# A planner that orders a two-layer encoder's instructions, given other durations and a convolution handed out one step at a time

## The chip, the cores and the metric

The kernel runs on one core of a Trainium2 chip. A core has TensorE (PE in the rows, with PEld for its weight loads), VectorE (DVE), ScalarE (ACT), GpSimd (POOL) and SyncE (SP), which here only issues DMAs. The metric is device time in microseconds of one execution; the kernel before has a median of 2336.31 over three runs.

## The reference

Two layers of a bidirectional encoder over 1024 tokens of width 1024. In each, five branches of width 256 run on the same normalised input, each is projected back to 1024 columns, weighted by a sigmoid gate and added, and the sum goes through an output projection. The branch that matters here is the convolution module:

```python
def conformer_branch(a, b, z, w_dw, b_dw, ln_g, ln_b):
    u = a * jax.nn.sigmoid(b)
    c = (depthwise_conv(u, w_dw) + b_dw.astype(u.dtype)).astype(F32)   # 31 taps
    mu = jnp.mean(c, axis=-1, keepdims=True)
    var = jnp.mean(jnp.square(c - mu), axis=-1, keepdims=True)
    n = (c - mu) * lax.rsqrt(var + EPS) * ln_g.astype(F32) + ln_b.astype(F32)
    return jax.nn.silu(n).astype(a.dtype) * jax.nn.silu(z)

for l in range(DEPTH):
    h = rmsnorm(x, norm_pre[l])
    ...                       # 18 projections of h; hgrn2, conformer, short conv, window and memory attention
    for n, yb in enumerate((y_hg, y_cf, y_sc, y_at, y_mem)):
        term = jax.nn.sigmoid(h @ w_gate[l, n]) * (yb @ w_branch[l, n])
        merged = term if merged is None else merged + term
    x = x + rmsnorm(merged @ w_out[l], norm_post[l])
```

## The kernel before

Channels lie on the 128 partitions, tokens along the free axis, in two halves of 512 (`s` is 0 or 1). A float32 product is made of three products of rounded parts (high by high, low by high, high by low), type float32r, each 128 rows by 512 columns: these are the split products. Scores, scan and value products of the attentions are plain float32 matmuls on 64 rows or 64 columns of the array, and transposes go through PE too.

All five engines run in the order in which the program emits, which the program decides while it is built. A main stream of items (projections, branch products, gates) emits one after the other on PE; beside it stand side generators (`plan.side`): recurrence, attention workers, convolution, preparation of gate operands. Class `Meter` (line 74 on) wraps each engine and gives every instruction an assumed duration, `cost`; class `Planner` keeps an assumed clock per engine and, per tile, when it was written and read. After each group of three products the main stream calls `plan.poll()`, which resumes every side generator that is due: `due` is the time at which its last piece is assumed to be seen (its end plus 0.2 us), or, for generators with `idle="DVE"`, the assumed end of VectorE's queue if that is later; it must not lie after PE's assumed clock. A generator emits up to its next `yield`. No instruction is timed by the plan on the chip; the durations only decide who stands before whom.

The convolution is such a generator with `idle="DVE"` (`conv` in `conformer_items`). For each of the two channel groups `j` it emits one tensor_scalar for the middle tap and 30 scalar_tensor_tensor, one per further tap, all on VectorE into `cf_c`; it yields after every odd tap, so two taps are emitted per resumption. Then come, for each half `s`, the sum over both groups (`cf_sum`), its split into `cf_muh` (ACT) and `cf_mul` (DVE), two products with a matrix of 1/256 (`cf_mu` on PE, the mean), the subtraction, squares on ACT, again a split and two products (`cf_var`), the root (ACT, with a table load), the reciprocal (DVE), a scale, a tanh (ACT, with a table load) and two more steps per group. The two halves are emitted one after the other. Only then the flag `cf` of the layer is set.

The main stream around it: `mem` (memory attention projections `ps_mq`, `ps_m_z`), `hz` (`ps_hz`), the first gate of branch 2 (`sc_g[:1]`, tiles `ps_g`), the products of branch 0 (`ps_b`), the three further gates (`sc_g[1:]`, 144 products into `ps_g`), and then `cz` (`ps_cz`), the projection whose SiLU multiplies the convolution's result. `cz` has `need=f"cf{l}"`: before its body the program calls `plan.wait`, which lets PE's assumed clock jump to the next due side piece until the flag is set. So whatever is left of the convolution's chain when the main stream reaches `cz` is emitted there, ahead of `ps_cz` on PE, with no other product between. After `cz` come branches 3, 1 and 4, then the gates as 7-product Strassen groups (`ps_gX`, `ps_gY`, `ps_gZ`), then the output projection.

Since `Meter` issues everything, nearly all rows carry one line number, L112; the tiles tell the rows apart.

Of the kernel before, what the change touches and what calls it, by code (L numbers as in the profile page):

```python
# [12 lines left out]
F32R = mybir.dt.float32r  # L13
# [62 lines left out]
class Meter:  # L76


    def __init__(self, engine, key, plan):
        self.engine, self.key, self.plan = engine, key, plan  # L80

    def __getattr__(self, name):
        f = getattr(self.engine, name)

        def call(*args, **kw):
            given = list(args) + [v for k, v in kw.items() if k not in ("out", "accum_out")]
            outs = [kw[k] for k in ("out", "accum_out") if k in kw]
            if "out" not in kw:
                outs.append(given.pop(0))
            tiles = [x for x in given if hasattr(x, "tensor")]  # L90
            n = prod(outs[0].shape[1:])
            if self.key == "PE":
                if name == "transpose":
                    cost = 0.107
                elif kw["rhs"].dtype == F32R:
                    cost = max(0.107, 0.00042 * n)
                else:
                    tiled = outs[0].shape[0] <= HD or kw["lhsT"].shape[0] <= HD
                    cost = max(0.085, 0.00167 * n) * (0.65 if tiled else 1.0)
            elif self.key == "DVE":  # L100
                n = max([n] + [prod(x.shape[1:]) for x in tiles])
                each = {"reciprocal": 0.0063, "tensor_scalar": 0.0006, "tensor_copy": 0.0006}.get(name, 0.00107)
                cost = (0.1 if name == "scalar_tensor_tensor" else 0.065) + n * each + 0.1 * ("accum_out" in kw)
            elif self.key == "ACT":
                cost = 0.055 + n * 0.00087 + 0.22 * ("accum_out" in kw) + self.plan.table(kw.get("func"))
            elif self.key == "DMA":
                cost = prod(outs[0].shape) * 1.12e-5
            else:
                cost = 0.05 + n * 0.0008 if name == "memset" else 0.5
            self.plan.add(self.key, cost, [x.tensor.name for x in outs],  # L110
                          [x.tensor.name for x in tiles])
            return f(*args, **kw)  # L112

        return call


class Planner:


    def __init__(self):  # L120
        self.t = dict.fromkeys(("PE", "DVE", "ACT", "POOL", "DMA"), 0.0)
        self.written, self.read = {}, {}
        self.last = 0.0
        self.flags = set()
        self.sides = []
        self.rings = {}
        self.loaded = None

    def add(self, key, cost, outs, ins):
        t = self.t[key]  # L130
# [76 lines left out]
def encoder(ctx: ExitStack, tc: tile.TileContext, a: dict, out: bass.AP):  # L207
# [398 lines left out]
    def conformer_items(l, hT, cs):  # L606
# [11 lines left out]
        def conv():  # L618
            yield f"at{l}01"
            for j in range(2):  # L620
# [6 lines left out]
                for k in range(CONFK):  # L627
                    if k == mid:
                        continue
                    o = k - mid  # L630
                    dst = c[:, max(0, -o):T - max(0, o)]
                    src = u[:, max(0, o):T - max(0, -o)]
                    dve.scalar_tensor_tensor(out=dst, in0=src, scalar=wt[:, j, k:k + 1], in1=dst,
                                             op0=ALU.mult, op1=ALU.add)
                    if k % 2:
                        yield
            for s in range(2):
                both = h2("cf_sum")
                dve.tensor_tensor(out=both, in0=cs[0][:, hs(s)], in1=cs[1][:, hs(s)], op=ALU.add)
# [23 lines left out]
            plan.flags.add(f"cf{l}")  # L663

        plan.side(conv(), idle="DVE")
        res = []
        for j in range(2):
# [895 lines left out]
```

## Time and profile before

| | us |
|---|---|
| median of 3 runs (2334.42 to 2337.20) | 2336.31 |
| the profiled execution's own time | 2335.37 |
| its span in the trace | 2333.6 |
| PE busy in the span | 2247.9 |
| DVE busy | 1644.3 |
| ACT busy | 996.4 |
| granted TensorE clock, mean share of full | 0.987 |

A matmul row's length counts its passage through the array, 0.39 us for 512 columns, while the next one starts 0.23 us later; what a product costs in a stream is the distance between starts. An engine's idle time stands in brackets behind a row, with what ended it.

### The profile page before, as it was taken

The numbers are of one execution on the slowest core, as the hardware profiler recorded it, in microseconds if no ns is written. First come the engines' busy times: TensorE is split into PE (matmuls) and PEld (weight loads), VectorE is DVE, ScalarE is ACT, GpSimd is POOL, SyncE is SP. The second block draws the span as 40 slices with busy tenths as digits, with TensorE's granted clock in tenths as the row PEclk, the third lists the DMA queues.
The fourth block names the chain that finished last, engine by engine and source line by source line (L and its number), as shares of the span: only waits on it lengthen the run. The fifth ranks groups of instructions, "written<-read, shape, count | busy, mean of one in ns | idle before, by whom it ended". The sixth has DMA issues, their size and how long they took to land.

```text
span 2333.6 us, 30426 instructions
## 1 busy us (share of the span) xinstructions
PE 2247.9 (96%) x11488; PEld 1837.7 (79%) x11488; DVE 1644.3 (70%) x2870; ACT 996.4 (43%) x1982; POOL 27.3 (1%) x41
## 2 busy tenths in 40 slices
PE   7999999989989999999999999999998999999998
PEld 6777788878767888887887878887786788888876
DVE  6767634788784887878667686266886768877765
ACT  5333344354455333335542424344544643333342
POOL 1000000000000000000110000000000000000000
PEclk9899999999999999999999999999999999999999
DMA  7102031101427333325450010411023463332244
GB/s 200 47 14 73 28 124 37 52 10 37 149 108 246 116 131 109 109 90 190 163 128 28 28 37 19 142 44 37 28 74 116 162 207 128 109 108 91 92 152 163
DMA packets 244563, 228.96 MB, mean 98 GB/s; under 512 B 29600, under 2 KB 190624, under 8 KB 244416
## 3 DMA queue, kind: packets, MB, share of 16 engines
q1 hardware_dynamic: 244416, 227.01, 29.7%
q8 instruction: 91, 1.49, 0.3%
q14 instruction: 56, 0.46, 0.1%
HBM read 173.49 MB, written 53.48 MB: 97 GB/s over the span
## 4 chain that ended last, share of the span: by engine, by line
PE 85%; DVE 8%; ACT 4%; issue 2%; DMA 0%; SPq 0%; POOL 0%; DVEq 0%; ACTq 0%; POOLq 0%
PE ps_gY L112 12%; PE ps_gX L112 8%; PE ps_b L112 8%; PE ps_gZ L112 8%; PE ps_o L112 7%; PE ps_hf L112 4%; PE ps_g L112 3%; PE h_s L112 3%; PE ps_cb L112 2%; PE ps_ca L112 2%; PE ps_hz L112 2%; PE ps_sc L112 2%; PE ps_sz L112 2%; PE ps_aq L112 2%; PE ps_at_z L112 2%
## 5 line engine op out<-in xcount | busy, mean ns | idle before, releaser
L112 DVE TENSOR_TENSOR lo<-raw_g,hi 128x512 fp32r<-128x512 f32 x232 | 159.0, 688 | 116.7 <-ACT hi L112 116.7
L112 ACT CAST hi<-raw_g 128x512 fp32r<-128x512 f32 x232 | 141.9, 616 | 60.5 <-PE ps_gY L112 56.2
L112 DVE SCALAR_TENSOR_TENSOR cf_c<-cf_u,cfw,cf_c 128x1009 f32<-128x1009 f32 (+14 forms) x120 | 152.9, 1274 | 2.7
L112 DVE TENSOR_TENSOR lo<-raw_in,hi 128x512 fp32r<-128x512 f32 x120 | 77.4, 686 | 94.9 <-ACT hi L112 94.8
L112 PE MATMUL ps_b<-yh,hi 128*128 128x512 f32 x320 | 125.9, 394 | 4.5 <-ACT pb_out L112 2.2
L112 PE MATMUL ps_b<-yl,hi 128*128 128x512 f32 x320 | 125.1, 391 | 1.4 <-DVE yl L112 1.4
L112 PE MATMUL ps_b<-yh,lo 128*128 128x512 f32 x320 | 124.7, 390 | 0.0
L112 ACT COPY pb_out<-ps_b 128x512 f32<-128x512 f32 x160 | 91.6, 590 | 77.3 <-PE ps_b L112 68.3
L112 ACT ACTIVATE g_e<-g_e 128x512 f32<-128x512 f32 x72 | 45.6, 634 | 161.3 <-DVE g_e L112 161.3
L112 PE MATMUL ps_gX<-h_0h,hi 128*128 128x512 f32 x288 | 112.1, 389 | 0.0
L112 PE MATMUL ps_gX<-h_0h,lo 128*128 128x512 f32 x288 | 112.1, 389 | 0.0
L112 PE MATMUL ps_gX<-h_0l,hi 128*128 128x512 f32 x288 | 112.0, 389 | 0.0
L112 PEld LDWEIGHTS h_s<-hQQ,hkp 64*128 64x128 f32 x896 | 60.9, 192 | 25.8 <-issue 18.2
L112 ACT CAST hi<-raw_in 128x512 fp32r<-128x512 f32 x120 | 68.8, 619 | 27.4 <-PE ps_ca L112 17.3
L112 PE MATMUL h_s<-hQQ,hkp 64*128 64x128 f32 x896 | 73.4, 298 | 6.4 <-DVE hQQ L112 2.5
L112 DVE TENSOR_TENSOR lo<-raw_wo,hi 128x512 fp32r<-128x512 f32 x64 | 42.2, 687 | 47.9 <-PE ps_o L112 28.5
L112 PEld LDWEIGHTS ps_b<-yh,hi 128*128 128x128 f32 x320 | 60.1, 188 | 19.7 <-ACT pb_out L112 4.0
L112 DVE COPY_PREDICATED hS<-masks,h_s 128x512 f32<-128x512 uint8 x112 | 75.3, 726 | 0.0
L112 PEld LDWEIGHTS ps_b<-yl,hi 128*128 128x128 f32 x320 | 60.1, 188 | 15.8 <-DVE yl L112 3.2
L112 ACT COPY hkp<-hK 128x512 f32<-128x512 f32 x56 | 37.2, 664 | 80.9 <-DVE hK L112 80.9
L112 PEld LDWEIGHTS ps_b<-yh,lo 128*128 128x128 f32 x320 | 60.1, 188 | 11.9
L112 ACT CAST hi<-raw_wo 128x512 fp32r<-128x512 f32 x64 | 37.8, 621 | 60.9 <-PE ps_o L112 47.0
(558 smaller groups left out, 6457.5 us busy)
## 6 DMA issues: line engine op xcount, KB each, us to landing
pb<-pb_out SPq DMA_DIRECT2D x160, 256.0 KB, 2.3
raw_g<-in_w_gate_dram SPq DMA_DIRECT2D x80, 512.0 KB, 3.6
pb<-pb SPq DMA_DIRECT2D x80, 512.0 KB, 5.2
raw_in<-in_w_in_dram SPq DMA_DIRECT2D x68, 512.0 KB, 3.8
raw_wo<-in_w_out_dram SPq DMA_DIRECT2D x32, 512.0 KB, 4.6
raw_b<-in_w_branch_dram SPq DMA_DIRECT2D x20, 512.0 KB, 4.1
x<-in_x_dram SPq DMA_DIRECT2D x8, 512.0 KB, 7.5
raw_mkv<-in_w_mem_kv_dram SPq DMA_DIRECT2D x8, 512.0 KB, 4.8
```

Source lines behind the costliest of these rows:

```text
L112: return f(*args, **kw)
```

## The change

Three of the assumed durations on PE change (split products from at least 0.107 us and 0.00042 us per column to 0.0135 + 0.000418 per column; plain matmuls from at least 0.085 to at least 0.212, tiled ones at 0.7 of it and no longer 0.65), and 0.09 us is added whenever a split product follows one that isn't, or the other way round. On VectorE the fixed part is larger for three kinds of instruction. And the convolution yields after every tap. No instruction is added, removed or altered by that; 27 loads of activation tables become 22, since these follow from the order on ScalarE.

```diff
             if self.key == "PE":
+                split = name != "transpose" and kw["rhs"].dtype == F32R
                 if name == "transpose":
                     cost = 0.107
-                elif kw["rhs"].dtype == F32R:
-                    cost = max(0.107, 0.00042 * n)
+                elif split:
+                    cost = 0.0135 + 0.000418 * n
                 else:
                     tiled = outs[0].shape[0] <= HD or kw["lhsT"].shape[0] <= HD
-                    cost = max(0.085, 0.00167 * n) * (0.65 if tiled else 1.0)
+                    cost = max(0.212, 0.00167 * n) * (0.7 if tiled else 1.0)
+                cost += 0.09 * (split != self.plan.split)
+                self.plan.split = split
             elif self.key == "DVE":
                 n = max([n] + [prod(x.shape[1:]) for x in tiles])
-                each = {"reciprocal": 0.0063, "tensor_scalar": 0.0006, "tensor_copy": 0.0006}.get(name, 0.00107)
-                cost = (0.1 if name == "scalar_tensor_tensor" else 0.065) + n * each + 0.1 * ("accum_out" in kw)
+                each = {"reciprocal": 0.0063, "tensor_scalar": 0.0005, "tensor_copy": 0.0006}.get(name, 0.00107)
+                fixed = {"scalar_tensor_tensor": 0.16, "tensor_scalar": 0.23, "copy_predicated": 0.12}.get(name, 0.07)
+                cost = fixed + n * each + 0.1 * ("accum_out" in kw)
...
         self.loaded = None
+        self.split = True
...
                     dve.scalar_tensor_tensor(out=dst, in0=src, scalar=wt[:, j, k:k + 1], in1=dst,
                                              op0=ALU.mult, op1=ALU.add)
-                    if k % 2:
-                        yield
+                    yield
```

What it moves, at three places (the helper's line is L116 in the changed program) of the first layer (the second has the same pattern at the first two). The first is PE at the gates of branch 2 (`ps_g`, operands `h_0h` and so on are the normalised input's parts) and the mean and variance products. Before, the first half's mean stands in the middle of a gate:

```order
L112 MATMUL ps_g_5432<-h_0l_111,hi 128x512
L112 MATMUL ps_g_5432<-h_0h_108,hi 128x512
L112 MATMUL ps_g_5432<-h_0h_108,lo 128x512
L112 MATMUL ps_g_5432<-h_0l_112,hi 128x512
L112 MATMUL cf_mu<-cf_muh,mean_w 128x512
L112 MATMUL cf_mu<-cf_mul,mean_w 128x512
L112 MATMUL ps_g_5432<-h_0h_108,hi 128x512
L112 MATMUL ps_g_5432<-h_0h_108,lo 128x512
```

Of the 144 products of these gates 81 stand behind that `cf_mu`, and 57 behind the first `cf_var`; only the second half's pairs stand between the last gate and `ps_cz`. With the change:

```order
L116 MATMUL ps_g_5520<-h_1h_260,lo 128x512
L116 MATMUL ps_g_5520<-h_1l_264,hi 128x512
L116 MATMUL cf_mu<-cf_muh,mean_w 128x512
L116 MATMUL cf_mu<-cf_mul,mean_w 128x512
L116 MATMUL cf_var<-cf_varh,mean_w 128x512
L116 MATMUL cf_var<-cf_varl,mean_w 128x512
L116 MATMUL cf_mu<-cf_muh,mean_w 128x512
L116 MATMUL cf_mu<-cf_mul,mean_w 128x512
L116 MATMUL cf_var<-cf_varh,mean_w 128x512
L116 MATMUL cf_var<-cf_varl,mean_w 128x512
L116 MATMUL ps_cz<-h_0h_106,hi 128x512
L116 MATMUL ps_cz<-h_0h_106,lo 128x512
```

Both halves' mean and variance products now stand behind the last gate, with nothing between them, ahead of `ps_cz`.

The second place is VectorE in the same stretch. `cf_c_4676` before and `cf_c_5106` now are the convolution of the second channel group, `mg` and `g_th` the merging of a gate with its branch, `lo` the low part of a weight. Before, the last taps and the first half's sum:

```order
L112 SCALAR_TENSOR_TENSOR cf_c_4676<-cf_u_3553,cfw_921,cf_c_4676 128x1011
L112 SCALAR_TENSOR_TENSOR cf_c_4676<-cf_u_3553,cfw_921,cf_c_4676 128x1010
L112 SCALAR_TENSOR_TENSOR mg_5031<-mg_5031,pb 128x512
L112 SCALAR_TENSOR_TENSOR cf_c_4676<-cf_u_3553,cfw_921,cf_c_4676 128x1009
L112 TENSOR_TENSOR cf_sum<-cf_c_3599,cf_c_4676 128x512
L112 TENSOR_TENSOR cf_mul<-cf_sum,cf_muh 128x512
L112 SCALAR_TENSOR_TENSOR mg_5075<-mg_5075,pb 128x512
L112 TENSOR_TENSOR lo<-raw_g_5355,hi 128x512 x2
```

Now the same sum and what stands ahead of it:

```order
L116 SCALAR_TENSOR_TENSOR g_th<-g_th,pb 128x512
L116 SCALAR_TENSOR_TENSOR cf_c_5106<-cf_u_3553,cfw_949,cf_c_5106 128x1011
L116 SCALAR_TENSOR_TENSOR cf_c_5106<-cf_u_3553,cfw_949,cf_c_5106 128x1010
L116 SCALAR_TENSOR_TENSOR cf_c_5106<-cf_u_3553,cfw_949,cf_c_5106 128x1009
L116 SCALAR_TENSOR_TENSOR g_th<-g_th,pb 128x512
L116 TENSOR_TENSOR lo<-raw_in_1920_5487,hi 128x512 x2
L116 TENSOR_TENSOR cf_sum<-cf_c_3596,cf_c_5106 128x512
L116 TENSOR_TENSOR cf_mul<-cf_sum,cf_muh 128x512
```

The last taps moved behind the merging of the fourth gate's first half, and the sum behind the merging of its second half, which needs the last gate product. Of this group's 30 further taps 18 stood behind the merging of the first gate's second half before, now 29 do.

The third place is PE in the projection `ps_hz`, beside the memory attention (`m_s` scores, `m_t` transposes, `m_o` products with the values, from two workers). Before:

```order
L112 MATMUL ps_hz<-h_1l_261,hi 128x512
L112 MATMUL m_t<-ident,m_p 128x128 x8
L112 MATMUL ps_hz<-h_1h_258,hi 128x512
L112 MATMUL ps_hz<-h_1h_258,lo 128x512
L112 MATMUL ps_hz<-h_1l_262,hi 128x512
L112 MATMUL m_o<-m_pT,mV_678 64x128 x8
L112 MATMUL ps_hz<-h_1h_258,hi 128x512
```

Now:

```order
L116 MATMUL ps_hz<-h_1l_261,hi 128x512
L116 MATMUL m_t<-ident,m_p 128x128 x4
L116 MATMUL ps_hz<-h_1h_258,hi 128x512
L116 MATMUL ps_hz<-h_1h_258,lo 128x512
L116 MATMUL ps_hz<-h_1l_262,hi 128x512
L116 MATMUL m_t<-ident,m_p 128x128 x4
L116 MATMUL m_o<-m_pT,mV_678 64x128 x4
L116 MATMUL ps_hz<-h_1h_258,hi 128x512
L116 MATMUL ps_hz<-h_1h_258,lo 128x512
L116 MATMUL ps_hz<-h_1l_262,hi 128x512
L116 MATMUL m_o<-m_pT,mV_678 64x128 x4
```

The two workers no longer stand side by side: runs of eight transposes and eight value products became two of four each. Over the whole program, runs of value products between other kinds go from 50 to 62, runs of transposes from 90 to 107, and those of the 64-row products (`h_s` and the like) stay at 57. The Strassen groups and the output projection keep their order on PE.

## Rows read from the trace of the kernel before

**Rows 1.** The page's span and busy time of each engine, and the first line of its chain of work that ended last, by engine.

```profile
span 2333.6 us, 30426 instructions
...
PE 2247.9 (96%) x11488; PEld 1837.7 (79%) x11488; DVE 1644.3 (70%) x2870; ACT 996.4 (43%) x1982; POOL 27.3 (1%) x41
...
PE 85%; DVE 8%; ACT 4%; issue 2%; DMA 0%; SPq 0%; POOL 0%; DVEq 0%; ACTq 0%; POOLq 0%
```

**Rows 2.** Busy time of each engine in stretches of the span; the columns are the stretch, its length, the engines with their instruction counts, the granted TensorE clock as a share of full, the DMA engines' share and GB/s. The recurrence lies in 20 to 310 and 1187 to 1457, the attentions in 460 to 570 and 1605 to 1716, the end of the convolution's chain in 640 to 665 and 1786 to 1812.

```profile
20.00:120.00 100.00, 92.60 (x583) 77.14 (x583) 69.67 (x140) 39.85 (x86) 3.73 (x6) 0.93 0.34 84
120.00:310.00 190.00, 183.26 (x1123) 145.58 (x1122) 134.42 (x240) 72.14 (x126) 0.00 (x0) 0.99 0.11 34
...
460.00:570.00 110.00, 102.29 (x635) 82.74 (x634) 85.74 (x210) 55.91 (x164) 0.00 (x0) 0.98 0.09 30
...
640.00:665.00 25.00, 17.14 (x60) 13.01 (x61) 17.10 (x23) 9.25 (x14) 0.00 (x0) 0.80 0.22 74
...
1187.00:1280.00 93.00, 90.51 (x596) 73.55 (x595) 69.11 (x122) 34.86 (x71) 4.88 (x4) 1.00 0.31 77
1280.00:1457.00 177.00, 170.53 (x1065) 138.34 (x1064) 125.72 (x224) 69.84 (x123) 0.00 (x0) 1.00 0.10 30
...
1605.00:1716.00 111.00, 104.12 (x634) 84.41 (x633) 86.75 (x214) 55.51 (x160) 0.00 (x0) 0.95 0.09 29
...
1786.00:1812.00 26.00, 17.92 (x64) 13.35 (x63) 17.43 (x24) 9.92 (x14) 0.00 (x0) 0.80 0.21 71
```

**Rows 3.** Instructions on PE in order of time, from the last gate product to the first product of `ps_cz`, first layer; columns are start, length, engine, line, operation, tiles, shapes, and in brackets the idle time before with what ended it.

```profile
639.11 0.39 PE L112 MATMUL ps_g<-h_1l,hi 128*128 128x512 f32 x1
644.45 0.79 PE L112 MATMUL cf_mu<-cf_muh,mean_w 128*128 128x512 f32 x1 [4.95 <-ACT cf_muh L112]
...
649.38 0.80 PE L112 MATMUL cf_var<-cf_varh,mean_w 128*128 128x512 f32 x1 [3.42 <-ACT cf_varh L112]
...
650.70 0.63 PE L112 MATMUL ps_cz<-h_0h,hi 128*128 128x512 f32 x1
```

**Rows 4.** The same view of VectorE, second half's sum to the end of the chain.

```profile
641.26 0.68 DVE L112 SCALAR_TENSOR_TENSOR g_th<-g_th,pb 128x512 f32<-128x512 f32 x1
...
643.06 0.68 DVE L112 TENSOR_TENSOR cf_sum<-cf_c,cf_c 128x512 f32<-128x512 f32 x1
...
650.94 0.69 DVE L112 TENSOR_SCALAR cf_rs<-cf_var 128x512 f32<-128x512 f32 x1 [0.89 <-PE cf_var L112]
...
662.03 0.69 DVE L112 SCALAR_TENSOR_TENSOR cf_c<-cf_t,cf_c 128x512 f32<-128x512 f32 x1
662.64 0.68 DVE L112 TENSOR_TENSOR b<-h_1h,h_1l 128x512 f32<-128x512 f32 x1
```

**Rows 5.** The same view of ScalarE; the first row is the tanh of the last gate.

```profile
639.94 0.57 ACT L112 ACTIVATE g_th<-ps_g 128x512 f32<-128x512 f32 x1
...
643.78 0.62 ACT L112 CAST cf_muh<-cf_sum 128x512 fp32r<-128x512 f32 x1 [2.24 <-DVE cf_sum L112]
...
656.48 1.28 ACT L112 ACT_TABLE_LOAD   x1 [4.19 <-DVE cf_c L112]
657.78 0.82 ACT L112 ACTIVATE cf_t<-cf_c,cfh 128x512 f32<-128x512 f32 x1
```

**Rows 6.** The same view of all engines where the first half's chain lies; `SPq` and `PEld` rows are left out.

```profile
613.97 0.69 DVE L112 TENSOR_TENSOR cf_sum<-cf_c,cf_c 128x512 f32<-128x512 f32 x1
...
620.07 0.39 PE L112 MATMUL cf_mu<-cf_muh,mean_w 128*128 128x512 f32 x1
...
620.53 0.39 PE L112 MATMUL ps_g<-h_0h,hi 128*128 128x512 f32 x1
...
625.97 0.39 PE L112 MATMUL cf_var<-cf_varh,mean_w 128*128 128x512 f32 x1
```

**Rows 7.** PE in order of time at the same place of the second layer.

```profile
1786.07 0.39 PE L112 MATMUL ps_g<-h_1l,hi 128*128 128x512 f32 x1
1791.12 0.79 PE L112 MATMUL cf_mu<-cf_muh,mean_w 128*128 128x512 f32 x1 [4.67 <-ACT cf_muh L112]
...
1796.05 0.80 PE L112 MATMUL cf_var<-cf_varh,mean_w 128*128 128x512 f32 x1 [3.41 <-ACT cf_varh L112]
```

**Rows 8.** Groups of instructions over the whole span: count, busy time, mean length of one in ns, idle time ahead of them.

```profile
L112 DVE TENSOR_TENSOR lo<-raw_g,hi 128x512 fp32r<-128x512 f32 x232 | 159.0, 688 | 116.7 <-ACT hi L112 116.7
L112 DVE SCALAR_TENSOR_TENSOR cf_c<-cf_u,cfw,cf_c 128x1009 f32<-128x1009 f32 (+14 forms) x120 | 152.9, 1274 | 2.7
...
L112 DVE SCALAR_TENSOR_TENSOR g_th<-g_th,pb 128x512 f32<-128x512 f32 x40 | 27.2, 681 | 0.6 <-ACT g_th L112 0.6
```

**Rows 9.** PE in order of time, a run of eight value products (16 rows of the trace, since a plain matmul leaves two) between split products.

```profile
547.98 0.40 PE L112 MATMUL ps_hz<-h_1l,hi 128*128 128x512 f32 x1
548.31 1.09 PE L112 MATMUL m_o<-m_pT,mV 128*64 128x128 f32 x16
549.34 0.50 PE L112 MATMUL ps_hz<-h_1h,hi 128*128 128x512 f32 x1
```

**Rows 10.** The same, a run of four value products in another place.

```profile
531.10 0.40 PE L112 MATMUL ps_m_z<-h_0l,hi 128*128 128x512 f32 x1
531.42 0.66 PE L112 MATMUL m_o<-m_pT,mV 128*64 128x128 f32 x8
532.01 0.50 PE L112 MATMUL ps_m_z<-h_1h,hi 128*128 128x512 f32 x1
```

## The prediction

> **What bounds the kernel now.** I read the page first: PE is busy in 2247.9 of 2333.6 us and holds 85% of the chain that ended last, DVE 8% [rows 1]. So time is made of PE's products plus the stretches in which PE stands still. The second view, busy time by stretch, shows where it stands: in the recurrence and the attentions it loses 2 to 8 us per stretch (7.4 in 20 to 120, 6.7 in 120 to 310, 7.7 in 460 to 570, 2.5 in 1187 to 1280, 6.5 in 1280 to 1457, 6.9 in 1605 to 1716, together 37.7), and in two short stretches it loses a third: 7.9 of 25 us and 8.1 of 26, with the granted clock down to 0.80 [rows 2]. The third view, PE in order of time, shows what these two are. After the last gate product PE waits for the mean of the convolution's second half, then for its variance, and `ps_cz` stands behind both [rows 3, 7]. The first half's same chain costs PE nothing: `cf_mu` and `cf_var` start there without idle time, between gate products [rows 6].
>
> The change adds no work. It moves instructions, so its price is a question of which wait is covered by which product.
>
> **The convolution emitted singly, and the new durations of VectorE.** A resumption of the convolution now gives one tap where it gave two, and the plan resumes it only when VectorE's assumed queue is empty and 0.2 us have passed since its last piece, while attention workers take the queue in between. So the taps drift back in the program: of the second group's 30 taps 29 instead of 18 stand behind the merging of the first gate's second half. With larger assumed times for a tap (1.256 us in place of 1.196 at 1024 elements) the plan also thinks VectorE occupied for longer. Consequence in the order on PE: the first half's mean and variance lose their cover of gate products and stand behind the last gate, ahead of the second half's. Built with the convolution's line alone the order already has all four pairs together there; with the durations alone the first `cf_mu` stands 48 products later than before, still among the gates. So the line with the `yield` is what decides.
>
> What it costs, in the first layer. A product holds PE for 0.23 us (two of them, from 620.07 to 620.53, take 0.46 [rows 6]). The last gate product starts at 639.11, so PE is free at 639.34; today the second half's `cf_mu` starts at 644.45, 5.11 later, and `cf_var` at 649.38, 4.93 after that [rows 3]. With the change those 5.11 and 4.93 are the first half's. Then its chain must run out before the second half's can begin, since both are emitted one after the other on VectorE and nothing else stands on PE. That stretch can be read from the second half now: from `cf_var` at 649.38 on PE through `cf_rs` at 650.94 to the next instruction on VectorE at 662.64, when the last `cf_c` is done, 13.26 us; then from `cf_sum` to `cf_mu`, 643.06 to 644.45, 1.39 us [rows 3, 4]. Behind it the second `cf_var` again takes 4.93. So between the gates' end and `ps_cz` there are 13.26 + 1.39 + 4.93 = 19.58 us more, less four products of 0.23 (0.91) that no longer stand among the gates: 18.67 us. The second layer has the same pair of waits (1786.07 to 1791.12 to 1796.05, again 4.93 for the second) [rows 7] and the same order, so 37.3 us for both.
>
> Two corrections. Today the last merging (`g_th`) starts at 641.26 although its tanh ended at 640.51 [rows 4, 5]: VectorE is still busy with the first half's chain, which won't stand there any more. That gives 0.75 per layer back, 1.5 in all. Against it stands VectorE's load ahead of that point: 29 taps of 1.274, five pairs of `lo` at 0.688 each, six mergings of 0.68 and 0.3 for one more make 36.9 + 6.9 + 4.1 + 0.3 = 48.2 us [rows 8], up to the merging of the last gate's first half. PE in the same time has 96 products of `ps_b` and 120 of the gates at 0.23 and a run of transposes and of value products (1.0), 50 us. So VectorE is on time by about 2 us; if that cover is gone, each us that it is late is a us of PE's standstill. I take the 1.5 off and keep +6 (3 per layer) as the upper end. The slow products after the wait (the clock of 0.80 in that stretch, [rows 2]) happen once per layer before as after and add nothing.
>
> In the exposed chain stands one table load for tanh, 1.28 us, and the tanh starts 1.30 after the load did [rows 5]; that is inside the 13.26. The Trainium skill (ScalarE: Activation LUTs, What ACT_TABLE_LOAD costs) puts a drain of some 1.38 us on top of each switch, which would make an exposed switch 1.4 longer and the two layers' sum 2.8 larger; the row shows no such drain.
>
> **The new durations of PE.** They move the side stages: workers of the memory attention that stood side by side come apart. A run of eight value products between split products holds PE for 549.34 - 547.98 - 0.23 = 1.13 us, a run of four for 532.01 - 531.10 - 0.23 = 0.68 [rows 9, 10], so cutting one in two costs 0.23. There are 12 more such runs: 2.8 us. The 17 additional runs of transposes have no row here; I bound a cut by 0 and the same 0.23, 0 to 4, and take 0, since a transpose uses the whole array as a split product does. The runs of 64-row products don't change in number.
>
> Whether the stages now meet their operands better or worse can't be priced from a trace that doesn't hold them. Nothing ties the sign: the order brings the scores' transposes closer to the scores at some places and the recurrence's value products farther from their states. The bounds are the idle time of the stretches: in the attentions 14.6 us, more or less; I take 0.
>
> **Sum.** 37.3 - 1.5 + 2.8 = 38.6 us. The profiled execution took 2335.4, 0.9 below the median of the three runs; its sum is 2374.0, and against the median 2336.3 + 38.6 = **2374.9**.
>
> **Rivals.** *Finer steps pay in the attentions.* A pair of taps holds VectorE for 2.5 us, a single one for 1.3 [rows 8], and an attention stage that comes due behind it waits that much less; also fewer taps stand in those stretches at all. If all idle time of both attention stretches went, it would be 38.6 - 14.6 = 24.0: 2360. For it: these stretches do lose 7.7 and 6.9. Against: VectorE is busy there in 86 of 110 us, not full, and half of such a stage's chain lies on ScalarE [rows 2]. The Trainium skill (Perfetto Trace Analysis, Optimizing Scalar/DVE Operations) states that where ScalarE or VectorE aren't saturated but cause bubbles on other engines, breaking up instructions may let work complete sooner; here emission is broken up rather than an instruction, and by that rule this rival would hold.
>
> *Tighter stages.* The plan now charges split products their full 0.227 us (0.215 before), so it lets a stage follow after fewer of them; where the true chain is longer than planned, PE waits more. The price is again bounded by what those stretches lose now: 38.6 + 14.6, 2389.5.
>
> *Not slower.* Truer durations remove the waits of the recurrence and the attentions nearly altogether. All six stretches lose 37.7; the balance is within 0.2% (4.7 us, about what a measurement of this kernel can tell from no change) from 33.9 on. With all of it gone: 2337.2. Against: the recurrence's stages are chains through VectorE and ScalarE, and no order shortens a chain.
>
> *The order isn't what PE does.* If PE took `ps_cz` ahead of the waiting `cf_mu`, whose operands have nothing to do with it, the chain would stay covered: 2336.3 + 2.8 = 2339. Today's rows speak against it: `ps_cz` needs only the normalised input and a weight, and yet starts at 650.70, behind both waits [rows 3].
>
> **How the numbers follow.** Forecast (2367 to 2383, by the corrections and half of the attentions' idle time either way) 0.70; finer steps pay 0.13; tighter stages 0.13; not slower 0.03; another order on PE 0.01. The range reaches into both middle rivals, 2358 to 2390, and leaves out the last two and the outer half of the middle ones. Faster by over 0.2% would need a gain beyond all idle time counted above: 0.01. Within 0.2%: 0.03. Slower: 0.96.
>
> **What would show it.** On PE behind the last gate product of each layer: four waits instead of two, of about 4.4, 4, 14 and 4 us, then `ps_cz`; the first half's `cf_mu` with idle time ahead of it where it has none now. The short stretches' idle time grows from 8 to about 26 us each, and ScalarE has 22 table loads. A first wait over 6 us would say that VectorE was late. The Strassen groups and the output projections should take what they take now. Wrong would be: the first half's pair covered, a gap between `cf_var` and the second `cf_mu` well under 13 us, or stretches of the recurrence or the attentions that shorten or lengthen by over 7 us each.

## The result, and the profile after

The changed kernel takes 2370.40 us (median of 4 runs, 2370.17 to 2372.28), the kernel before beside it 2335.74: 1.015 times as long, 95% interval 1.0132 to 1.0168, or 34.7 us more. The profiled execution took 2370.17, its span is 2368.4 against 2333.6. The prediction was 2374.9 (2358 to 2390).

First the page of the changed kernel: busy time by engine, and the chain that ended last.

```profile
PE 2254.6 (95%) x11488; PEld 1837.0 (78%) x11488; DVE 1647.6 (70%) x2870; ACT 992.2 (42%) x1977; POOL 28.0 (1%) x41
...
PE 82%; DVE 10%; ACT 5%; issue 2%; DMA 0%; SPq 0%; POOL 0%; DVEq 0%; ACTq 0%; POOLq 0%
```

No work was added: PE has the same 11488 instructions, and its rows cover 6.7 us more (a row's length counts its passage, and rows overlap less where products stand apart). The other 28 us of the span are time in which PE stands still, and DVE and ACT enter the chain with 10 and 5% where they had 8 and 4 [rows 1].

Busy time by stretch, changed kernel, columns as in [rows 2]; the stretches are those of the recurrence, the attentions and the end of the convolution's chain, at their new places.

```profile
118.70:305.30 186.60, 181.35 (x1107) 143.62 (x1106) 132.20 (x235) 68.02 (x122) 0.00 (x0) 1.00 0.12 35
454.90:568.00 113.10, 104.51 (x646) 83.20 (x645) 78.29 (x210) 58.80 (x170) 0.00 (x0) 0.97 0.09 29
636.90:667.00 30.10, 6.00 (x10) 2.48 (x10) 17.64 (x23) 11.36 (x16) 0.00 (x0) 0.57 0.18 61
1297.00:1473.00 176.00, 170.55 (x1064) 138.57 (x1063) 126.01 (x223) 67.21 (x120) 0.00 (x0) 1.00 0.10 30
1620.00:1732.00 112.00, 104.09 (x635) 82.72 (x635) 77.53 (x213) 57.96 (x166) 0.00 (x0) 0.95 0.09 29
1803.70:1834.00 30.30, 6.15 (x11) 2.65 (x11) 17.84 (x24) 11.35 (x16) 0.00 (x0) 0.58 0.19 61
```

The two short stretches are lost time now: 24.1 and 24.2 us without PE, where they lost 7.9 and 8.1 [rows 2], at a granted clock of 0.57 and 0.58. The recurrences (first and fourth line) lose 5.3 and 5.5, 1.5 and 1.0 less than in [rows 2]; the attentions (second and fifth) 8.6 and 7.9, 0.9 and 1.0 more.

PE in order of time from the last gate product to `ps_cz`, first layer, and behind the last "..." the second layer:

```profile
636.73 0.39 PE L116 MATMUL ps_g<-h_1l,hi 128*128 128x512 f32 x1
640.99 0.55 PE L116 MATMUL cf_mu<-cf_muh,mean_w 128*128 128x512 f32 x1 [3.87 <-ACT cf_muh L116]
...
645.93 0.79 PE L116 MATMUL cf_var<-cf_varh,mean_w 128*128 128x512 f32 x1 [3.42 <-ACT cf_varh L116]
...
660.62 0.79 PE L116 MATMUL cf_mu<-cf_muh,mean_w 128*128 128x512 f32 x1 [13.17 <-ACT cf_muh L116]
...
665.60 0.80 PE L116 MATMUL cf_var<-cf_varh,mean_w 128*128 128x512 f32 x1 [3.46 <-ACT cf_varh L116]
...
666.92 0.63 PE L116 MATMUL ps_cz<-h_0h,hi 128*128 128x512 f32 x1
667.35 0.63 PE L116 MATMUL ps_cz<-h_0h,lo 128*128 128x512 f32 x1
...
1803.50 0.39 PE L116 MATMUL ps_g<-h_1l,hi 128*128 128x512 f32 x1
1807.76 0.50 PE L116 MATMUL cf_mu<-cf_muh,mean_w 128*128 128x512 f32 x1 [3.87 <-ACT cf_muh L116]
...
1812.56 0.79 PE L116 MATMUL cf_var<-cf_varh,mean_w 128*128 128x512 f32 x1 [3.42 <-ACT cf_varh L116]
...
1827.25 0.79 PE L116 MATMUL cf_mu<-cf_muh,mean_w 128*128 128x512 f32 x1 [13.18 <-ACT cf_muh L116]
...
1832.24 0.80 PE L116 MATMUL cf_var<-cf_varh,mean_w 128*128 128x512 f32 x1 [3.46 <-ACT cf_varh L116]
...
1833.56 0.63 PE L116 MATMUL ps_cz<-h_0h,hi 128*128 128x512 f32 x1
```

These answer to [rows 3, 7]. Four waits stand where there were two. From the end of the last gate product's turn (636.73 + 0.23) the mean comes 4.03 us later, its variance 4.94 after that, the second mean 14.69 after the first variance, the second variance 4.98 after its mean. From the last gate product's start to `ps_cz` it is 30.19 us in the first layer and 30.06 in the second; before it was 11.59 and 11.3.

VectorE in the same stretch, which answers to [rows 4]:

```profile
637.79 0.69 DVE L116 SCALAR_TENSOR_TENSOR g_th<-g_th,pb 128x512 f32<-128x512 f32 x1 [0.94 <-ACT g_th L116]
...
639.60 0.68 DVE L116 TENSOR_TENSOR cf_sum<-cf_c,cf_c 128x512 f32<-128x512 f32 x1
...
647.49 0.69 DVE L116 TENSOR_SCALAR cf_rs<-cf_var 128x512 f32<-128x512 f32 x1 [0.89 <-PE cf_var L116]
...
658.57 0.69 DVE L116 SCALAR_TENSOR_TENSOR cf_c<-cf_t,cf_c 128x512 f32<-128x512 f32 x1
659.18 0.69 DVE L116 TENSOR_TENSOR cf_sum<-cf_c,cf_c 128x512 f32<-128x512 f32 x1
```

The last merging (637.79) starts as soon as its tanh is there, VectorE having stood idle for 0.94 us, and no longer behind the chain's first half; the first half's chain then runs from 639.60 to 659.18 without any product of PE beside it but its own. On ScalarE the load of the tanh's table is still 1.28 us and the tanh starts 1.29 after it, as in [rows 5]:

```profile
653.03 1.28 ACT L116 ACT_TABLE_LOAD   x1 [4.19 <-DVE cf_c L116]
654.32 0.81 ACT L116 ACTIVATE cf_t<-cf_c,cfh 128x512 f32<-128x512 f32 x1
```

Where the 34.8 us of span came from, by first starts on PE in both traces (us, before to after):

| from ... to | layer 1 | layer 2 |
|---|---|---|
| last `ps_g` to first `ps_cz` (the chain) | 11.6 to 30.2 | 11.3 to 30.1 |
| first `ps_mq` to last `ps_g` (memory attention, `ps_hz`, branch 0, gates) | 184.9 to 187.6 | 186.1 to 188.1 |
| start to first `ps_ak` (layer 2: `ps_hi` to `ps_ak`; recurrence) | 305.1 to 300.4 | 266.3 to 266.0 |
| first `ps_gX` to last `ps_gY` (Strassen groups) | 342.5 to 342.5 | 342.5 to 342.5 |

The output projection of the second layer is 1.6 shorter besides; small shifts make up the rest.

### The profile page after: what moved, and what is told of

It is laid out like the page before. It is cut to its first block, busy times and chain, and to the rows that moved or that the text cites. A ratio compares the mean times of both kernels' runs of the same rounds, so it can differ in the third digit from the quotient of the medians.

```text
span 2368.4 us, 30445 instructions
## 1 busy us (share of the span) xinstructions
PE 2254.6 (95%) x11488; PEld 1837.0 (78%) x11488; DVE 1647.6 (70%) x2870; ACT 992.2 (42%) x1977; POOL 28.0 (1%) x41
## 4 chain that ended last, share of the span: by engine, by line
PE 82%; DVE 10%; ACT 5%; issue 2%; DMA 0%; SPq 0%; POOL 0%; DVEq 0%; ACTq 0%; POOLq 0%
PE ps_gY L116 12%; PE ps_b L116 9%; PE ps_gX L116 8%; PE ps_gZ L116 8%; PE ps_o L116 7%; PE ps_hf L116 4%; PE ps_g L116 4%; PE h_s L116 2%; PE ps_hz L116 2%; PE ps_cb L116 2%; PE ps_ca L116 2%; PE ps_sz L116 2%; PE ps_aq L116 2%; PE ps_at_z L116 2%; PE ps_hq L116 2%
## 5 line engine op out<-in xcount | busy, mean ns | idle before, releaser
L116 DVE TENSOR_TENSOR lo<-raw_g,hi 128x512 fp32r<-128x512 f32 x232 | 159.0, 688 | 121.0 <-ACT hi L116 120.9
L116 ACT CAST hi<-raw_g 128x512 fp32r<-128x512 f32 x232 | 141.9, 615 | 59.2 <-PE ps_gY L116 56.2
L116 DVE SCALAR_TENSOR_TENSOR cf_c<-cf_u,cfw,cf_c 128x1009 f32<-128x1009 f32 (+14 forms) x120 | 153.0, 1275 | 2.4
L116 DVE TENSOR_TENSOR lo<-raw_in,hi 128x512 fp32r<-128x512 f32 x120 | 77.4, 686 | 82.4 <-ACT hi L116 82.0
L116 ACT COPY pb_out<-ps_b 128x512 f32<-128x512 f32 x160 | 92.1, 589 | 89.2 <-PE ps_b L116 82.6
L116 PE MATMUL ps_b<-yl,hi 128*128 128x512 f32 x320 | 125.5, 392 | 2.6 <-DVE yl L116 2.6
L116 PE MATMUL ps_b<-yh,hi 128*128 128x512 f32 x320 | 126.1, 394 | 1.3 <-DVE th_cz L116 1.1
L116 PE MATMUL ps_b<-yh,lo 128*128 128x512 f32 x320 | 125.3, 392 | 1.0 <-DVE lo L116 1.0
L116 ACT ACTIVATE g_e<-g_e 128x512 f32<-128x512 f32 x72 | 45.6, 634 | 161.4 <-DVE g_e L116 161.4
L116 PE MATMUL ps_gX<-h_0h,hi 128*128 128x512 f32 x288 | 112.0, 389 | 0.0
L116 PE MATMUL ps_gX<-h_0h,lo 128*128 128x512 f32 x288 | 112.0, 389 | 0.0
L116 PE MATMUL ps_gX<-h_0l,hi 128*128 128x512 f32 x288 | 112.0, 389 | 0.0
L116 ACT CAST hi<-raw_in 128x512 fp32r<-128x512 f32 x120 | 69.1, 619 | 45.4 <-PE ps_ca L116 17.3
L116 PEld LDWEIGHTS h_s<-hQQ,hkp 64*128 64x128 f32 x896 | 60.2, 188 | 23.6 <-issue 13.8
L116 PE MATMUL h_s<-hQQ,hkp 64*128 64x128 f32 x896 | 72.9, 295 | 5.0 <-DVE hS L116 3.0
L116 DVE COPY_PREDICATED hS<-masks,h_s 128x512 f32<-128x512 uint8 x112 | 75.3, 727 | 0.0
L116 DVE TENSOR_TENSOR lo<-raw_wo,hi 128x512 fp32r<-128x512 f32 x64 | 42.2, 688 | 47.3 <-PE ps_o L116 28.5
L116 PEld LDWEIGHTS ps_b<-yl,hi 128*128 128x128 f32 x320 | 60.4, 189 | 16.7 <-DVE yl L116 4.1
L116 ACT COPY hkp<-hK 128x512 f32<-128x512 f32 x56 | 37.2, 664 | 86.1 <-DVE hK L116 86.1
L116 PEld LDWEIGHTS ps_b<-yh,hi 128*128 128x128 f32 x320 | 60.4, 189 | 15.4 <-DVE th_cz L116 1.8
L116 PEld LDWEIGHTS ps_b<-yh,lo 128*128 128x128 f32 x320 | 60.5, 189 | 13.8 <-DVE lo L116 1.4
L116 ACT CAST hi<-raw_wo 128x512 fp32r<-128x512 f32 x64 | 37.8, 620 | 60.1 <-PE ps_o L116 45.5
```

## The experiments

Two theories stood against each other. **The chain**: the time is the first half's chain that lost its cover, and whatever else the order does is small. **The plan**: finer steps and other durations make the stages of the recurrence and the attentions meet their operands differently, and the 35 us are the sum of many such shifts. Every ratio is against the kernel before, run on the same chip beside it.

**The first half held back by itself** (edit of the kernel before, with pairs of taps and old durations).

```diff
@@ conv, ahead of the two halves
+            yield f"gates{l}"
             for s in range(2):
@@ main stream
+                sc_g[3].flag = f"gates{l}"
```

> The kernel before, with one thing changed: the convolution's side generator waits, ahead of the first half's sum, for a flag that the last gate of branch 2 sets. Durations and the yield after every second tap stay, and on PE only the first half's mean and variance products change their place: they stand behind the last gate, as in the changed kernel. Theory (the exposed normalisation chain is the whole price): the short stretch from the last gate to ps_cz grows from 11.6 to about 30 us in each layer, 35 us in all, about 2371. Rival (the new durations move the recurrence's and the attentions' stages to worse places, and the chain is hidden or absorbed later): about 2336 to 2342, since these stages don't move here.

Measured: 2370.90, ratio 1.0150 (1.0135 to 1.0166). PE in order of time:

```profile
637.16 0.39 PE L112 MATMUL ps_g<-h_1l,hi 128*128 128x512 f32 x1
641.42 0.80 PE L112 MATMUL cf_mu<-cf_muh,mean_w 128*128 128x512 f32 x1 [3.87 <-ACT cf_muh L112]
...
646.35 0.79 PE L112 MATMUL cf_var<-cf_varh,mean_w 128*128 128x512 f32 x1 [3.42 <-ACT cf_varh L112]
...
661.05 0.79 PE L112 MATMUL cf_mu<-cf_muh,mean_w 128*128 128x512 f32 x1 [13.17 <-ACT cf_muh L112]
...
666.03 0.80 PE L112 MATMUL cf_var<-cf_varh,mean_w 128*128 128x512 f32 x1 [3.46 <-ACT cf_varh L112]
...
667.35 0.63 PE L112 MATMUL ps_cz<-h_0h,hi 128*128 128x512 f32 x1
```

The same four waits, and 30.19 us from the last gate to `ps_cz` as in the changed kernel, with PE's order otherwise that of before. The chain alone makes the whole difference; the plan's other shifts aren't needed for it.

**The `yield` alone** (kernel before, a yield after every tap).

```diff
-                    if k % 2:
-                        yield
+                    yield
```

> The kernel before with the convolution's line alone: a yield after every tap, durations as before. Theory: the order puts all four pairs behind the last gate, so the stretch to ps_cz is about 30 us again and the time is 2336 + 35.5, give or take 4 for attention stages that meet other taps: 2367 to 2375. Rival (the durations are what costs): within 5 us of 2336. Second rival (single taps shorten waits in the attentions): the two attention stretches lose less than half of the 7.7 and 6.9 us that they lose before, so 2360 or less.

Measured: 2370.69, ratio 1.0152 (1.0137 to 1.0168). From the last gate to `ps_cz` 31.5 us in both layers. Finer steps do help the attentions: `ps_mq` to `ps_hz` is 5.4 and 6.6 us shorter; `ps_hz` to the first `ps_b` is 2.9 longer and the rest up to the last gate 2.0 shorter. That is the mechanism of the rival "finer steps pay": from `ps_mq` to the last gate 4.5 and 5.7 us a layer, of which 0.9 are products that went with the chain, so 3.6 and 4.8. Its price is that the taps which leave these stretches push the chain behind the gates, 20 us a layer.

**The durations alone** (changed kernel with pairs of taps).

```diff
-                    yield
+                    if k % 2:
+                        yield
```

> The changed kernel with the yield after every second tap again, new durations kept. The first cf_mu stands among the gate products, 33 of them behind it, the first cf_var with 9 products between it and the second cf_mu. Theory: 9 products cover 2 us of the 14.65 from the first cf_var to the second cf_mu, so 12.6 us are exposed where 5.1 were, 7.5 us more per layer: 2336 + 15 - 5 for the recurrence (whose order is that of the changed kernel) = 2346, between 2341 and 2352. Rival (the durations are what costs): near 2370.

Measured: 2344.84, ratio 1.0040 (1.0025 to 1.0055). The first half stays among the gates; the second half's mean comes later:

```profile
634.33 0.39 PE L116 MATMUL ps_g<-h_1l,hi 128*128 128x512 f32 x1
646.13 0.79 PE L116 MATMUL cf_mu<-cf_muh,mean_w 128*128 128x512 f32 x1 [11.42 <-ACT cf_muh L116]
...
651.07 0.80 PE L116 MATMUL cf_var<-cf_varh,mean_w 128*128 128x512 f32 x1 [3.42 <-ACT cf_varh L116]
...
652.39 0.63 PE L116 MATMUL ps_cz<-h_0h,hi 128*128 128x512 f32 x1
```

11.57 us of wait for the mean where [rows 3] has 5.11. So some +6.5 a layer from the chain, and the recurrence of the first layer gives 6.1 back. `ps_mq` to `ps_hz` is 3.3 and 4.9 shorter than before. The single taps of the changed kernel, which are all that this kernel lacks, lengthen that stretch again, by 5.4 and 6.3; under the old durations they had shortened it by 5.4 and 6.6.

**Which durations** (both with pairs of taps; first PE's new ones with VectorE's old, then PE's old ones with VectorE's new).

```diff
@@ changed kernel, to PE's durations alone; the other kernel is the one before with the lines marked - in place of the + ones
-                fixed = {"scalar_tensor_tensor": 0.16, "tensor_scalar": 0.23, "copy_predicated": 0.12}.get(name, 0.07)
-                cost = fixed + n * each + 0.1 * ("accum_out" in kw)
+                cost = (0.1 if name == "scalar_tensor_tensor" else 0.065) + n * each + 0.1 * ("accum_out" in kw)
...
-                    yield
+                    if k % 2:
+                        yield
```

> Pairs of taps, the new durations of PE with the charge for a change of kind, the old durations of VectorE. In its order the first half's cf_mu and cf_var stand in branch 0's products, the second half's cf_mu 92 products behind that cf_var, its cf_var 26 on, still ahead of the last gate's end. Theory: the whole chain is covered at the old place of ps_cz: 2336 - 21, less some 5 for the recurrence if it is PE's durations that moved it: 2310 to 2318. Rival (what is gained there is lost in attention stages that the durations move): 2330 or more.

> Pairs of taps, the old durations of PE, the new ones of VectorE. In its order all four pairs stand behind the last gate, as in the changed kernel, though the taps come in pairs. Theory: the place alone sets the price: 2336 + 35, between 2362 and 2375. Rival (single taps have a price of their own): near 2345, as in the run with both durations and pairs.

Measured: PE's alone 2330.77, ratio 0.9979 (0.9970 to 0.9989); VectorE's alone 2378.04, ratio 1.0182 (1.0165 to 1.0199). With PE's the chain is covered whole, 0.2 us from the last gate to `ps_cz`, which saves 11.4 and 11.1; `ps_cz` itself takes 1.7 less, since its first products no longer run at the lower clock. But the gain of 13 a layer goes back elsewhere: recurrence (`ps_hi` to `ps_ak`) +1.4 and +5.7, attentions (`ps_mq` to `ps_hz`) +5.7 and +3.9, from there to the first `ps_b` +2.0 and +2.3. The waits on PE in the first layer's recurrence (120 to 310) and attentions (449 to 584), in us, times and longest, in this kernel:

```profile
PE h_o L115 <- DVE h_st L115: 7.4, 4, 2.1
...
PE at_t L115 <- DVE at_p L115: 5.0, 3, 3.5
```

and in the kernel before:

```profile
PE h_o L112 <- DVE h_st L112: 3.6, 4, 1.1
...
PE at_t L112 <- DVE at_p L112: 2.0, 2, 1.7
```

The scan's products wait twice as long for their states (7.4 us for 3.6). With VectorE's durations alone it is the other way round: recurrence -7.1 and -4.4, attentions -10.8 and -9.1, and from the last gate to `ps_cz` 37.0 us, more than in the changed kernel. There PE waits 10.7 us for the first mean, since five taps are still to run on VectorE behind the last gate:

```profile
634.37 6.50 DVE L113 SCALAR_TENSOR_TENSOR cf_c<-cf_u,cfw,cf_c 128x1013 f32<-128x1013 f32 x5
640.90 0.69 DVE L113 TENSOR_TENSOR cf_sum<-cf_c,cf_c 128x512 f32<-128x512 f32 x1
```

So a VectorE that the plan takes to be later, and not the `yield` alone, moves the chain: the two sets of durations pull it in opposite directions, and the changed kernel has both plus the single taps. Both times lie above the expected ranges. The first is 13 us above the end of its range, by what the plan gave back, and its rival (gained here, lost in attention stages) is what came; the second is 3 us above, by the taps left over.

**Taps by fours** (kernel before).

```diff
-                    if k % 2:
+                    if k % 4 == 3:
```

> The kernel before with a yield after every fourth tap in place of every second, all else as before. In its order the whole chain stands ahead of the last gate's end, at the old place of ps_cz: 150 products between the first cf_var and the second cf_mu, 26 up to the second cf_var. Theory: the piece of work that a resumption hands out sets how early the convolution ends, so fours do the opposite of singles: 11.4 us per layer at the gates' end and 1.7 of slow products go, 26 in all, and some of it is lost where four taps (5.1 us on VectorE) stand ahead of an attention stage: 2312 to 2328. Rival (larger pieces hurt the attentions more than they hide): above 2336.

Measured: 2328.86, ratio 0.9968 (0.9956 to 0.9981), 0.9 above the expected range and well under the rival's 2336. The chain is covered again (-11.4, -11.1, and `ps_cz` -1.7), and `ps_b` to the last gate grows by 9.0 and 9.4. Stretches of this kernel, memory attention and then branch 0 with the gates:

```profile
454.00:544.00 90.00, 78.60 (x465) 63.52 (x464) 70.53 (x166) 45.18 (x124) 0.00 (x0) 0.92 0.11 36
582.00:649.50 67.50, 66.05 (x345) 53.98 (x344) 47.04 (x84) 38.10 (x78) 0.00 (x0) 1.00 0.38 129
```

The same two of the kernel before:

```profile
454.00:540.00 86.00, 78.29 (x495) 63.15 (x494) 64.32 (x172) 48.56 (x135) 0.00 (x0) 0.98 0.10 32
581.00:639.30 58.30, 58.30 (x276) 48.04 (x275) 46.29 (x60) 26.16 (x49) 0.00 (x0) 1.00 0.45 149
```

The attention has 30 PE rows fewer and yet takes 4 us longer, with 11.4 us idle for 7.7; the gates have 69 rows more, since 16 scores, 16 transposes and 16 value products of the memory attention came to stand there, almost without waits (1.5 us). So coarser steps delay the attention workers: their waits stay behind and their work moves.

**The consumer moved instead.** If the chain's end is the price, `ps_cz` should stand behind other products. First `cz` behind branches 3 and 4 in the changed kernel; branch 1's operand is then split before the last items of `cz` have multiplied the convolution's result, so this kernel leaves that gating out of part of branch 1.

```diff
-... + sc_g[1:] + cz
+... + sc_g[1:]
                 yield from branch_items(l, 3, y_at, pbd[3], need=f"at{l}")
-                yield from branch_items(l, 1, y_cf, pbd[1]) + branch_items(l, 4, y_mem, pbd[4], need=f"mem{l}")
+                yield from branch_items(l, 4, y_mem, pbd[4], need=f"mem{l}") + cz
+                yield from branch_items(l, 1, y_cf, pbd[1])
```

> The changed kernel with the items of ps_cz moved behind the products of branches 3 and 4, so that the main stream reaches the wait for the convolution 192 products (43.6 us) later; branch 1, which needs ps_cz, comes last. In its order 78 products stand between the first cf_var and the second cf_mu. Theory: the chain of 4.3 + 4.9 + 14.65 + 4.9 us is covered in both layers, so 2370 - 2 x 28 = 2314, up to 2322 where the gates' operands or branch 1 now come late. Rival (something else than the chain costs, VectorE is the bound there): the wait moves with ps_cz or comes back ahead of branch 1 or of the Strassen groups, and the time stays above 2360.

Measured: 2327.91, ratio 0.9963 (0.9949 to 0.9978), 14 above what was expected. From the last gate to the first `ps_gX` it is 91.5 us, which is all that was hoped for, but the Strassen groups take 10.9 and 9.5 us longer. PE's waits there:

```profile
PE ps_gY L116 <- ACT T2h L116: 7.3, 1, 7.3
```

The operands of the Strassen gates are made by a side generator that waits for the convolution's flag and, for the second half of them, for one that the last item of `cz` sets. Now they come late (the cast of the last `T2h` starts at 738.13, 34.6 us behind the last `ps_cz`): part of the wait moved there.

Then `cz` behind branch 3 alone and branch 4 ahead of branch 1, in the changed kernel, in the kernel before, and in the changed kernel with pairs of taps.

```diff
-... + sc_g[1:] + cz
-                yield from branch_items(l, 3, y_at, pbd[3], need=f"at{l}")
-                yield from branch_items(l, 1, y_cf, pbd[1]) + branch_items(l, 4, y_mem, pbd[4], need=f"mem{l}")
+... + sc_g[1:]
+                yield from branch_items(l, 3, y_at, pbd[3], need=f"at{l}") + cz
+                yield from branch_items(l, 4, y_mem, pbd[4], need=f"mem{l}") + branch_items(l, 1, y_cf, pbd[1])
```

> The changed kernel with the items of ps_cz moved behind the products of branch 3 only, followed by branch 4 and then branch 1. In its order 36 products stand between the last gate and the first cf_mu, 32 up to the first cf_var, 30 up to the second cf_mu, none up to the second cf_var. Theory: at 0.227 us each they cover all of the first two waits and 6.8 of the 14.65 us of the third; 7.8 + 4.9 us stay exposed where 28 were, 16 less per layer: 2370 - 32 = 2338, from 2333 to 2346. Rival (a wait that is moved comes back ahead of the Strassen groups, as part of it did in the run before): 2350 or more.

> The kernel before, durations and pairs of taps as they were, with ps_cz behind the products of branch 3, then branch 4 and branch 1. In its order 96 products stand between the first cf_var and the second cf_mu, 33 up to the second cf_var, 24 behind that. Theory: the two waits that the kernel before still shows (11.5 us of stretch per layer, of which 0.9 is work) are covered too: 2336 - 21 = 2315, from 2312 to 2322 where some of it comes back. Rival (VectorE is what binds there): above 2330.

> The changed kernel's durations, pairs of taps, and ps_cz behind the products of branch 3, then branch 4 and branch 1: the run with both durations and the moved ps_cz in one. In its order 74 products stand between the first cf_var and the second cf_mu, 11 up to the second cf_var, none behind. Theory: all waits but 2.4 us of the last are covered, and the recurrence keeps what the durations gave it (6 us in the first layer, under 1 in the second): 2336 - 29 for the move - 6 + 5 = 2306, between 2301 and 2313. Rival (the durations' gain in the recurrence is chance of one profile): 2312 or more.

Measured: in the changed kernel 2345.38, ratio 1.0041 (1.0026 to 1.0056); in the kernel before **2306.90, ratio 0.9876 (0.9861 to 0.9890)**, faster than both kernels by 29 and 63 us; in the changed kernel with pairs 2318.37, ratio 0.9922 (0.9908 to 0.9937).

In the kernel before with `cz` moved, the stretch from the last gate to `ps_cz`, first layer:

```profile
639.60:662.40 22.80, 22.80 (x102) 18.69 (x101) 13.15 (x18) 15.37 (x27) 0.00 (x0) 1.00 0.64 218
```

PE is full there at full clock, and `ps_cz` starts without a wait, its products 0.23 us apart:

```profile
662.17 0.39 PE L112 MATMUL ps_b<-yl,hi 128*128 128x512 f32 x1
662.39 0.39 PE L112 MATMUL ps_cz<-h_0h,hi 128*128 128x512 f32 x1
662.62 0.39 PE L112 MATMUL ps_cz<-h_0h,lo 128*128 128x512 f32 x1
```

From the last gate to the first `ps_gX` it takes 90.29 us where it took 105.04, 14.75 less: 10.45 of wait, 1.70 in `ps_cz`, whose first products had run at the lower clock, and 2.6 in the branches' products, whose idle time fell from 3.2 to 1.2. The last two are what the expected 2315 had left out.

In the changed kernel the edit takes 13.3 of the chain's 18.6 a layer away, and waits of 9.5 us for the second mean and 3.5 for its variance remain: 96 products of branch 3 are about 22 us, and two chains one after the other take longer. With pairs the time is 5 us above the expected range. It isn't the rival's reason, a gain in the recurrence by chance: from the start to the first `ps_ak` it takes 298.5 us, 6.6 less than before, so that gain is there again. But it is 99.1 us from the last gate to `ps_gX`, some 9 more than the 90.3. More than half of that lies behind `ps_cz`; waits of PE in 681 to 732 there:

```profile
PE ps_b L116 <- DVE lo L116: 1.7, 1, 1.7
PE ps_b L116 <- ACT yh L116: 1.4, 1, 1.4
PE ps_b L116 <- DVE yl L116: 1.2, 1, 1.2
```

Branch 4's operands are late: on VectorE they stand behind the gate operands that begin when the chain has ended, and the chain, which VectorE's new durations start later, ends later than PE's products need it. I read this off the rows; no run takes it apart.

## Why the prediction was right, step by step

**The exposed chain** (37.3 less 1.5, 35.8). Right: 18.60 and 18.75 from the last gate to `ps_cz`, less the four products (0.91) a layer that left the gates, 35.5. Each piece was near: waits of 4.03, 4.94, 14.69 and 4.98 in starts where about 4.4, 4.9, 14.7 and 4.9 had been worked out from [rows 3, 4]. The first half's chain took what the second half's took before, since the same instructions stand in the same in-order queues. It is shown alone by the first experiment.

**VectorE on time by about 2 us.** That it is on time was right: the first wait is shorter than before's 5.11, and VectorE stands idle for 0.94 us ahead of the last merging. The upper end of +6 was a real danger: with VectorE's durations alone five taps were left behind the last gate, 10.7 us of wait.

**Cut runs** (2.8). Right in size, on a stretch that holds more. From `ps_mq` to the last gate, with the 0.91 added back, the layers grew by 3.6 and 2.9. From `ps_hz` to the last gate no row of PE has idle time in either kernel, and there each layer takes 1.56 more (99.95 and 0.91 for 99.30), 3.1 in all, near the 2.8; no run takes the cuts alone. By the median distances between starts, a cut run of value products costs 0.20 and not 0.23 (0.327 ahead of a run and 0.209 behind it, in place of 0.109 and 0.227), and a cut run of transposes gives 0.08 back (0.232 and 0.028 for 0.109 and 0.227), where the prediction took 0. The other 2.1 and 1.4 lie from `ps_mq` to `ps_hz`, where PE's idle time grew by 0.9 and 1.0; they belong to the next term.

**Stages of the recurrence and the attentions** (0, bounded by their idle time). The sum was small, as taken, but by luck. It is a balance of shifts of 1 to 11 us with opposite signs: PE's durations lengthen recurrence and attentions, VectorE's shorten them, and the two together leave the first layer's recurrence 6.1 shorter. The single taps turn their sign: "finer steps pay" was a true mechanism under the old durations (3.6 and 4.8 us a layer), which ran beside the exposed chain instead of in its place; on top of the new durations single taps lengthen `ps_mq` to `ps_hz` by 5.4 and 6.3. So these effects don't add up, and why the sign turns no run shows. In the changed kernel the recurrences came out 4.7 and 0.3 shorter, the second output projection 1.6 and small shifts 0.7; against that, `ps_mq` to the last gate took 3.7 more than forecast. With 0.3 less from the chain that leaves the span 3.8 under the forecast sum; the other 0.7 of the 4.5 lies between the profiled executions and the medians.

**"The line with the `yield` is what decides".** True of the two halves of the change as I had parted them: the `yield` alone gives 1.0152, the durations alone 1.0040. Too simple as a cause: VectorE's durations alone, with pairs, bring the same four waits, the first of them longer, and 1.0182.

**Table loads.** 22, as the order says; what five fewer are worth no run takes apart. The tanh's in the exposed chain costs 1.29 us from its start to the tanh's. The root's load, which the prediction doesn't count, starts at 645.89 beside the variance products and ends at 647.17, while the root waits for VectorE until 648.21, so it costs nothing. The drain that the Trainium skill (ScalarE: Activation LUTs, What ACT_TABLE_LOAD costs) puts on top does not show there, nor where ScalarE had just been at work: at 175.81 a load starts 0.02 us behind the end of an ACTIVATE, and the next one starts 0.01 us behind the load's end, at 177.10.

**The rivals.** *Tighter stages* is what PE's durations did by themselves (+5.7 and +3.9 in the attentions); with VectorE's beside them these stretches were 3.3 and 4.9 shorter than before. *Not slower* fails: the changed kernel still loses 5.3 to 8.6 us in each of the four stretches shown. *Another order on PE* fails: `ps_cz`, which needs nothing of the chain, starts right behind the last `cf_var` and not ahead of it. The 1.6 us in the output projection of the second layer, which the prediction had left as it was, can't be put down to the change: it takes 89.2 us there and 90.7 before, 89.1 to 89.7 in five of the ten other kernels and 90.7 to 91.3 in the other five, with no edit common to either group.

## What to carry to other kernels

When a planner's numbers change, look for the chain through other engines that the main engine's in-order queue must pass, and count the independent products that the new order leaves between its links; here two links that lost them cost 35 us, and all other shifts together came to about nothing, by luck. The cure is to move the consumer that nobody waits for behind products that are free (29 us), after asking which later operands hang on the same flag. Truer durations are no gain by themselves: the two sets of this change, taken singly, gave 0.998 and 1.018.

## What the runs showed of the hardware

A wait costs more than itself. In the first layer of the changed kernel PE ran ten products in the 30.1 us from 636.9 to 667; the granted clock is 0.57 there and still 0.50 from 666 to 671, the lower of its two levels, 1.2 GHz instead of 2.4. The first `ps_cz` products start 0.43 us apart (666.92, 667.35) instead of 0.23. All of `ps_cz` takes 24.0 and 22.7 us in the two layers of the changed kernel, 23.2 and 23.3 in the kernel before, and 21.5 in the four kernels in which no wait stands ahead of it. So the price is about the same for 11 us of waits as for 30, and of the 13 us a layer that a covered chain gives back, 1.7 come from TensorE's clock.

The chain through three engines repeats closely: its long stretch, from the first `cf_var` to the second `cf_mu`, took 14.69 us in both layers of the changed kernel and 14.70 in both where the first half alone was held back.

What a plain value product of the attention costs depends on where it stands: by the median starts of all traces here, it follows another one after 0.109 us and a split product after 0.327, and a split product follows it after 0.209.
